# Loading the residual between its first stores, and the values' products four units behind the scores

## The chip, the cores and the metric

The kernel runs on one core of a Trainium2 chip. The metric is the time of one execution in microseconds on the device, here the median of several runs. A second execution under the hardware profiler gives the busy times, waits and clocks that are quoted.

## The reference

A two-layer encoder over 1024 tokens of width 1024, all in float32. The first layer begins with grouped-query attention (16 heads of 64, 4 key/value heads), then come cross-attention into 256 memory tokens and a gated MLP; the second layer has a pooling mixer in place of the attention. Every sub-layer is normed first and added to the residual. The parts that matter here:

```python
def attend_block(q_blk):
    scores = jnp.einsum('bkgqd,bksd->bkgqs', q_blk, kt).astype(jnp.float32)
    p = jax.nn.softmax(scores, axis=-1).astype(vt.dtype)
    return jnp.einsum('bkgqs,bksd->bkgqd', p, vt)
...
x = x + axial_gqa_attention(rmsnorm(x, attn_norm[ia]), attn_w_qkv[ia], ...)
x = x + memory_cross_attention(rmsnorm(x, xattn_norm[i]), rmsnorm(mem, mem_norm[i]), ...)
```

## The kernel before

Matrix products run on TensorE (PE) with every operand split into a high and a low float32r part: ScalarE (ACT) makes the high part by a copy, VectorE (DVE) the low part by a subtraction, and three matmuls (`mm3`, L746 to L748) are added up.

*The attention loop.* There are 128 units, one for each head and each block of 128 queries; two neighbouring units form a pair. Per unit:

- `scores`: four matmuls (L779) into a score buffer `pA` (two of them), the row maximum on DVE (L789), the exponential on ACT (L792), the reciprocal of the sum on DVE (L794) and the scaling of the weights on GpSimd (POOL, L795).
- `turn_p`: eight transposes of the scaled weights on TensorE (L740) into two `pB` buffers (four of them), and the split into `PT` by ACT (L673) and DVE (L674).
- `values`, once a pair: sixteen matmuls (L1192, L1193), a copy on ACT (L1198), a DMA that moves half of it across partitions (`crossed`, L1200), an addition on POOL (L1202) and, for every second pair, two more POOL instructions (L1205, L1206).

`skewed` writes these three stages step by step, each with its lag in units; the tile scheduler then lays out each engine's queue from that program order and from when it holds operands to be ready. In the projection and what follows it the program order is the queue order.

*The loop's end.* The output weight `attn_w_o` is loaded in eight pieces through the `scr` buffers (`load_rows`, `load_w`, L681) that the attention weights also use, and each is split. The residual X (eight row tiles of 128 x 1024) is loaded from the input, 512 KB a tile (L2128). All these DMAs are issued by SP, one after the other; one that has to wait holds up those behind it.

*The projection.* `begin` walks over 16 steps (n, t), n the half of the columns, t the row tile: (0,0), (0,2), (1,0), (1,2), (0,4), (1,4), (0,6), (1,6), (0,1), (1,1), and so on. Each has a product (`gemm`, 24 matmuls), a call of `free(n, t)`, the addition to X on DVE (L1556), and a store of that half tile of X to DRAM (`save`, L314, tensor `Xq`). After the second half of a tile its norm factor is computed on ACT and POOL (L727, L719, L721), and DVE's norm (L318) overwrites X in place, with `gain`, a row broadcast to all partitions (`bcast`, L712). The norm therefore waits for both stores of its tile to land. Between the steps stand the transposes of normed tiles (`turn`, L323): tile 0 behind the product (1,2), tile 2 behind (0,4).

Of the kernel before, what the change touches and what calls it, by code (L numbers as in the profile page):

```python
# [16 lines left out]
P = 128  # L17
# [62 lines left out]
def skewed(n, *stages):  # L80

    for step in range(n + max(lag for lag, _ in stages)):
        for lag, stage in stages:
            if 0 <= step - lag < n:
                stage(step - lag)
# [212 lines left out]
class Seven:  # L298
# [71 lines left out]
    def load(self, f, j):  # L370

        c = self.columns(f)[j]
        src = self.w[:, c:c + P].rearrange("(k p) n -> p k n", p=P)
        self.nc.sync.dma_start(out=self.raws[f][j].rearrange("p (k n) -> p k n", k=NK), in_=src)
# [254 lines left out]
class Kernel:  # L629
# [132 lines left out]
    def attention(self):  # L762
        nc, R, a, tc = self.nc, self.R, self.a, self.tc
# [4 lines left out]
        units = [(j, hh, i) for j in range(NT // 2) for hh in range(NH) for i in range(2)]  # L768
# [401 lines left out]
        with tc.tile_pool(name="at", bufs=1, reuse_waits="tile") as at:  # L1170
            PT = [[at.tile([P, 2048], F32R, name=f"PT{i}{j}") for j in range(2)] for i in range(2)]
            halves = self.scr().rearrange("p (a b c) -> p a b c", a=2, b=2)
            def parts(u):
                return (x.rearrange("p (a b) -> p a b", a=8) for x in PT[u // 2 % 2])

            def turn_p(u):
                ph, pl = parts(u)
                c = slice(u % 2 * P, (u % 2 + 1) * P)
                self.transposed(prs.pop(u), lambda g, p: self.hi_lo(ph[:, 4 * g:4 * g + 4, c], pl[:, 4 * g:4 * g + 4, c], p))

            def values(u):
                j, hh, i = units[u]
                if i == 0:
                    return
                kv = hh // 4
                if hh == 0:
                    OT.append([R.get(), R.get()])
                ph, pl = parts(u)
                o = self.psB()[:, :256]
                for kt in range(NT):  # L1190
                    v = R.tiles[V[kt // 4]].rearrange("p (k h c) -> p k h c", k=4, h=4)[:, kt % 4, kv, :]
                    nc.tensor.matmul(o, v, ph[:, kt], start=kt == 0, stop=False)  # L1192
                    nc.tensor.matmul(o, v, pl[:, kt], start=False, stop=kt == NT - 1)  # L1193
                odd, pair = hh % 2, u // 4 % 2
                if not odd:
                    sums["crossed"] = at.tile([P, 256], F32, name="crossed", bufs=2)
                own, far = halves[:, pair, odd], sums["crossed"]
                nc.scalar.copy(own, o)  # L1198
                mine, other = (slice(HD * odd, HD * odd + HD), slice(HD - HD * odd, P - HD * odd))
                nc.sync.dma_start(out=far[mine], in_=own[other])  # L1200
                total = halves[:, pair, 0]
                nc.gpsimd.tensor_tensor(out=total[mine], in0=own[mine], in1=far[mine], op=OP.add)  # L1202
                if odd:
                    hi, lo = (R.v(x, 8)[:, hh // 2] for x in OT[j])
                    nc.gpsimd.tensor_scalar(hi, total, 1.0, 1.0, op0=OP.mult, op1=OP.mult)  # L1205
                    nc.gpsimd.tensor_tensor(out=lo, in0=total, in1=hi.bitcast(F32), op=OP.subtract)  # L1206
                if hh % 4 == 3:
                    if j % 2:
                        R.put(Q[kv, j // 2])

            skewed(len(units), (0, scores), (2, turn_p), (3, values))
            R.put(*V, *K[0], *K[1])
        return OT

# [5 lines left out]

        return (self.R.hv(h).rearrange("p (k n) -> p k n", k=4)[:, k % 4, cols] for h in hs[k // 4 * 2:k // 4 * 2 + 2])

    def cross(self, i, X, steps=None, mixer=None, over={}):

        nc, R, a = self.nc, self.R, self.a
        Xd = self.tc.dram_tile([S, D], F32, name=f"Xq{i}")
        U = Seven(self, a["xattn_w_q"][i], lambda f: (2 * f * P, (2 * f + 1) * P), X, Xd, self.bcast(a["xattn_norm"][i]))
        plan_sums = self.down_sums(i)  # L1230
        q, nf, mem, kT, v, sm, PT, O, wo = {}, D // (2 * P), {}, [], [], {}, {}, {}, {}
        both = lambda t: [(f"X{t}", j) for j in range(2)]
# [6 lines left out]
        def plan_split(plan, name, f, late):  # L1239
# [3 lines left out]
            def high():  # L1243
                hs = q[c] = R.get_halves(1)
                nc.scalar.activation(R.hv(hs[0]), U.bank[f][name], AF.Copy, scale=XHD ** -0.5)

            def low():
                h, l = (R.hv(x) for x in q[c])
                nc.vector.scalar_tensor_tensor(l, U.bank[f].pop(name), XHD ** -0.5, h.bitcast(F32), op0=OP.mult, op1=OP.subtract)
            ins = [(u, 0), (u, 1)]  # L1250
# [184 lines left out]
        def main():  # L1435
            order = U.order(nf)
            if steps:
                U.begin(*steps, lambda: None)
                U.H["T4"] = [R.get(), R.get()]
                over.update({"DVE": 6.5, "ACT": 4.9})  # L1440
            plan = Plan(R, over, {"scr": 2 if steps else 6, "A": 2, "B": 4, "half": len(R.freed)})
            if mixer:
                mixer(plan, U, X)
                order[:4] = [(2, 0), 3, (1, 0), 5, (2, 1), None]
# [673 lines left out]
    def run(self):  # L2118
        nc, R, a = self.nc, self.R, self.a
        OT = self.attention()  # L2120
        ws = [self.load_rows(a["attn_w_o"][0], 0)]
        xp = self.ctx.enter_context(self.tc.tile_pool(name="xres", bufs=1, reuse_waits="tile"))
        X = [xp.tile([P, D], F32, name=f"X{t}") for t in range(NT)]
        for t in (0, 2, None, 4, 6, 1, 3, 5, 7):
            if t is None:
                ws.append(self.load_rows(a["attn_w_o"][0], 1))
            else:
                nc.sync.dma_start(out=X[t], in_=a["x"][0][t * P:(t + 1) * P, :])  # L2128

        def lhs(t, k):  # L2130
            return (R.v(s, 8)[:, k, t % 4 // 2 * P:(t % 4 // 2 + 1) * P] for s in OT[t // 4 * 2 + t % 2])

        def free(t):
            if t % 4 >= 2:
                R.put(*OT[t // 4 * 2 + t % 2])

        steps = self.rows_by(lhs, X, free, lambda n, k: self.blk(ws[n], k, slice(0, 512)), lambda n: R.put(*ws[n]))
        lhs, *ops = self.cross(0, X, steps)
        ready = []
        gemm, add, over = self.ffn(0, lhs, X, *ops, lambda plan: ready.extend([self.pool_weights(plan)]))  # L2140
        lhs, *ops = self.cross(1, X, None, partial(self.pool_mixer, gemm, add, ready[0]), over)
        self.ffn(1, lhs, X, *ops, out=self.out[0])


# [30 lines left out]
```

## Time and profile before

| | us |
|---|---|
| median of 3 runs | 2509.69 (2505.69 to 2514.07) |
| the profiled execution, its time | 2508.51 |
| its span, first to last instruction | 2506.7 |
| TensorE busy | 2473.4 (99%) |
| VectorE busy | 1958.6 (78%) |
| ScalarE busy | 1348.4 (54%) |
| GpSimd busy | 436.2 (17%) |
| mean granted clock of TensorE | 0.998 |

The times in rows of the profile are microseconds from the first instruction of the span. A row of the timeline has start, duration, engine, line, operation, what is written and read; in brackets stands how long the engine was idle before it and what ended the wait. A row of the waits has who waited for whom, the total, the number of times and the longest. Matmuls overlap in a pipeline, so from one start to the next is the better measure of them than the duration. The attention loop lies between about 175 and 529 us, the projection behind it.

### The profile page before, as it was taken

What the parts mean: (1) busy time and instruction counts of PE and PEld (TensorE: products, weight loads), DVE (VectorE), ACT (ScalarE), POOL (GpSimd) and SP (SyncE); (2) the same over time, 40 slices, a digit from 0 to 9 for tenths busy, and PEclk for the clock granted to TensorE, in tenths of its full rate; (3) what the DMA queues carried; (4) which work ended last, traced back from release to release, by engine and by line L of the source; (5) the groups of instructions that cost most, each with busy time, mean ns of one, the idle gap of its engine ahead of it and who ended that gap; (6) DMA issues with size and microseconds to landing.
All of it is one profiled execution on the core that took longest, in us unless ns stands there. A gap on an engine that the chain in (4) does not pass through costs nothing.

```text
span 2506.7 us, 37225 instructions
## 1 busy us (share of the span) xinstructions
PE 2473.4 (99%) x13435; PEld 2129.7 (85%) x13435; DVE 1958.6 (78%) x2899; ACT 1348.4 (54%) x2307; POOL 436.2 (17%) x594
## 2 busy tenths in 40 slices
PE   9999999999999999999999999999999999999998
PEld 8999999978898888888888888889888888887887
DVE  7779989864986379888889776987559888888875
ACT  6558888852655255555555334655335555554542
POOL 5756666631011000000000003102010000000001
PEclk9999999999999999999999999999999999999999
DMA  7100000042595124243258553388223324337852
GB/s 253 43 2 14 13 14 13 13 171 68 187 317 183 57 79 126 84 122 110 85 170 285 198 182 111 126 283 306 73 72 109 114 84 124 108 93 255 278 189 97
DMA packets 314733, 326.50 MB, mean 130 GB/s; under 512 B 14133, under 2 KB 248861, under 8 KB 314549
## 3 DMA queue, kind: packets, MB, share of 16 engines
q1 hardware_dynamic: 314549, 324.12, 39.9%
q8 instruction: 106, 1.74, 0.3%
q14 instruction: 78, 0.64, 0.1%
HBM read 232.48 MB, written 82.58 MB: 126 GB/s over the span
## 4 chain that ended last, share of the span: by engine, by line
PE 87%; issue 4%; DVE 3%; DMA 2%; ACT 2%; POOL 1%; SPq 0%; POOLq 0%; DVEq 0%; ACTq 0%
PE pB L746 21%; PE pB L748 21%; PE pB L747 21%; PE pA L779 4%; PE pB L740 4%; PE pA L748 3%; PE pA L746 3%; PE pA L747 3%; PE pB L1193 2%; PE pB L1192 2%; DVE R L668 1%; PE pB L323 1%; ACT R L665 1%; DMA scr<-in_ffn_w_down 1%; PE pA L2058 1%
## 5 line engine op out<-in xcount | busy, mean ns | idle before, releaser
L746 PE MATMUL pB<-R,R 128*128 128x512 f32 (+1 forms) x2764 | 1024.3, 371 | 8.4 <-DVE scr L439 3.3
L748 PE MATMUL pB<-R,R 128*128 128x512 f32 (+1 forms) x2760 | 1016.4, 368 | 1.3 <-DVE R L668 1.2
L747 PE MATMUL pB<-R,R 128*128 128x512 f32 (+1 forms) x2764 | 1017.3, 368 | 0.0
L746 PEld LDWEIGHTS pB<-R,R 128*128 128x128 f32 x2764 | 521.1, 189 | 100.7 <-DVE scr L439 4.6
L748 PEld LDWEIGHTS pB<-R,R 128*128 128x128 f32 x2760 | 520.1, 188 | 89.0 <-DVE R L668 2.6
L747 PEld LDWEIGHTS pB<-R,R 128*128 128x128 f32 x2764 | 521.2, 189 | 85.6 <-DVE R L674 0.4
L665 ACT ACTIVATE R<-scr 128x512 fp32r<-128x512 f32 (+2 forms) x340 | 256.9, 781 | 218.3 <-DMA scr<-Gs 60.3
L668 DVE TENSOR_TENSOR R<-scr,R 128x512 fp32r<-128x512 f32 (+2 forms) x340 | 291.6, 887 | 21.5 <-ACT R L665 20.9
L668 DVE TENSOR_TENSOR R<-X,R 128x512 fp32r<-128x512 f32 x374 | 252.5, 686 | 67.5 <-ACT R L665 66.6
L665 ACT ACTIVATE R<-X 128x512 fp32r<-128x512 f32 x374 | 231.7, 630 | 135.8 <-PE pB L747 65.4
L719 POOL TENSOR_SCALAR ms<-ss 128x1 f32<-128x1 f32 (+1 forms) x53 | 14.9, 281 | 1659.0 <-ACT R L727 1280.7
L437 ACT COPY scr<-pB 128x512 f32<-128x512 f32 x156 | 91.3, 585 | 188.3 <-PE pB L748 182.5
L673 ACT ACTIVATE PT<-pB 128x512 fp32r<-128x512 f32 x256 | 140.1, 604 | 56.0 <-PE pB L740 55.7
L789 DVE TENSOR_REDUCE nm<-pA 128x1 f32<-128x1024 f32 x125 | 152.5, 1220 | 20.5 <-PE pA L779 20.5
L674 DVE TENSOR_TENSOR PT<-pB,PT 128x512 fp32r<-128x512 f32 x256 | 163.5, 679 | 5.0 <-ACT PT L673 4.9
L1765 DVE TENSOR_TENSOR X<-pB,X 128x512 f32<-128x512 f32 (+1 forms) x145 | 99.3, 686 | 85.5 <-PE pB L748 84.5
L795 POOL TENSOR_SCALAR scr<-scr,inv 128x1024 f32<-128x1024 f32 x125 | 140.7, 1127 | 70.1 <-DVE inv L794 69.8
L746 PE MATMUL pA<-R,R 128*128 128x512 f32 (+1 forms) x420 | 150.6, 359 | 0.0
L748 PE MATMUL pA<-R,R 128*128 128x512 f32 (+1 forms) x420 | 150.2, 358 | 0.2 <-DVE R L668 0.2
L747 PE MATMUL pA<-R,R 128*128 128x512 f32 (+1 forms) x420 | 150.0, 357 | 0.0
L779 PE MATMUL pA<-R,R 128*128 128x512 f32 x512 | 145.4, 405 | 0.0
L792 ACT ACTIVATE scr<-pA,nm 128x1024 f32<-128x1024 f32 x125 | 139.8, 1118 | 1.5 <-DVE nm L789 0.5
(172 smaller groups left out, 3485.0 us busy)
## 6 DMA issues: line engine op xcount, KB each, us to landing
X<-in_ffn_w_up SPq DMA_DIRECT2D x82, 512.0 KB
Gs<-X SPq DMA_DIRECT2D x105, 256.0 KB
scr<-in_ffn_w_down SPq DMA_DIRECT2D x45, 512.0 KB
scr<-Gs SPq DMA_DIRECT2D x35, 512.0 KB
scr<-in_xattn_w_kv SPq DMA_DIRECT2D x32, 512.0 KB
scr<-Gs SPq DMA_DIRECT2D x42, 384.0 KB
Wt<-scr SPq DMA_DIRECT2D x44, 256.0 KB
Gs<-scr SPq DMA_DIRECT2D x42, 256.0 KB
```

The source lines that it names most:

```text
L665: self.nc.scalar.activation(hi, src, AF.Copy)
L668: self.nc.vector.tensor_tensor(out=lo, in0=src, in1=hi.bitcast(F32), op=OP.subtract)
L673: nc.scalar.activation(hi, src, AF.Copy)
L674: nc.vector.tensor_tensor(out=lo, in0=src, in1=hi.bitcast(F32), op=OP.subtract)
L740: self.nc.tensor.transpose(p[:, k, :], src[:, b * P:(b + 1) * P], self.ident)
L746: mm(out, ah, bh, start=start, stop=False)
L747: mm(out, ah, bl, start=False, stop=False)
L748: mm(out, al, bh, start=False, stop=stop)
L779: nc.tensor.matmul(s[:, kh * 512:(kh + 1) * 512], q, R.v(K[part][kh], 4)[:, kv], start=part == 0, stop=part == 1)
L789: nc.vector.tensor_reduce(nm, s, axis=AX.X, op=OP.max, negate=True)
L792: nc.scalar.activation(pr, s, AF.Exp, bias=nm, accum_out=rs)
L795: nc.gpsimd.tensor_scalar(pr, pr, ri, 1.0, op0=OP.mult, op1=OP.mult)
```

## The change

Two edits. In the loop, `values` stands four units behind the scores instead of three, and within a step it comes before `turn_p`. In the order of the program a pair was scores, transposes, scores, transposes, values; it becomes scores, transposes, scores, values, transposes.

For the residual, tiles 0, 2 and 4 are loaded up front as before (with the gain row now in front of tile 4, where it came behind all loads), and tiles 6, 1, 3, 5 and 7 are loaded one at a time out of `free`, that is between the product of a step and its store: behind the products (1,2), (0,4), (1,4), (1,6) and (0,1). The rest of the diff passes the gain row into `cross`.

```diff
-            skewed(len(units), (0, scores), (2, turn_p), (3, values))
+            skewed(len(units), (0, scores), (4, values), (2, turn_p))
...
-    def cross(self, i, X, steps=None, mixer=None, over={}):
+    def cross(self, i, X, gain, steps=None, mixer=None, over={}):
...
-        U = Seven(self, a["xattn_w_q"][i], lambda f: (2 * f * P, (2 * f + 1) * P), X, Xd, self.bcast(a["xattn_norm"][i]))
+        U = Seven(self, a["xattn_w_q"][i], lambda f: (2 * f * P, (2 * f + 1) * P), X, Xd, gain)
...
-        for t in (0, 2, None, 4, 6, 1, 3, 5, 7):
-            if t is None:
-                ws.append(self.load_rows(a["attn_w_o"][0], 1))
-            else:
-                nc.sync.dma_start(out=X[t], in_=a["x"][0][t * P:(t + 1) * P, :])
+
+        def load(t):
+            nc.sync.dma_start(out=X[t], in_=a["x"][0][t * P:(t + 1) * P, :])
+        load(0)
+        load(2)
+        ws.append(self.load_rows(a["attn_w_o"][0], 1))
+        gain = self.bcast(a["xattn_norm"][0])
+        load(4)
+        later = {(1, 2): 6, (0, 4): 1, (1, 4): 3, (1, 6): 5, (0, 1): 7}
...
-        steps = self.rows_by(lhs, X, free, lambda n, k: self.blk(ws[n], k, slice(0, 512)), lambda n: R.put(*ws[n]))
-        lhs, *ops = self.cross(0, X, steps)
+        gemm, add, freed = self.rows_by(lhs, X, free, lambda n, k: self.blk(ws[n], k, slice(0, 512)), lambda n: R.put(*ws[n]))
+
+        def between(n, t):
+            freed(n, t)
+            if (n, t) in later:
+                load(later[n, t])
+        steps = gemm, add, between
+        lhs, *ops = self.cross(0, X, gain, steps)
...
-        lhs, *ops = self.cross(1, X, None, partial(self.pool_mixer, gemm, add, ready[0]), over)
+        lhs, *ops = self.cross(1, X, self.bcast(a["xattn_norm"][1]), None, partial(self.pool_mixer, gemm, add, ready[0]), over)
```

## The prediction

> **What bounds the kernel now.** I read the page first (busy shares, the chain of waits), then what TensorE waits for over the whole span, then the two places that the change touches, as windows and as instructions in order of time.
>
> ```profile
> span 2506.7 us, 37225 instructions
> PE 2473.4 (99%) x13435; PEld 2129.7 (85%) x13435; DVE 1958.6 (78%) x2899; ACT 1348.4 (54%) x2307; POOL 436.2 (17%) x594
> PE pB L323 <- DVE X L318: 3.9, 2, 3.5
> PE pB L740 <- POOL scr L795: 3.0, 5, 1.0
> ```
>
> TensorE is busy 99% of the span, so an edit without fewer matmuls can win only idle time of TensorE. All its waits are short. The two longest groups that the change can reach are the transposes of the normed residual (L323), which once wait 3.5 us for VectorE's norm, and the transposes of the attention weights (L740), which five times wait for GpSimd's scaling (L795), 3.0 us together. That is the size of the prize: some 7 us, 0.3%, which is also about the least that a measurement of this kernel tells from no change. The half-clock stretch below is the only other loss there.
>
> The windows of the attention loop and of the stretch behind it (columns: stretch, length, then busy time of PE, PEld, DVE, ACT, POOL, then granted clock, DMA share, GB/s) and a list of TensorE's waits from 186 to 516 us:
>
> ```profile
> 281.00:362.00 81.00, 81.00 (x596) 74.44 (x595) 73.41 (x119) 68.65 (x133) 51.72 (x59) 1.00 0.05 13
> 484.00:491.00 7.00, 6.14 (x44) 5.29 (x43) 6.15 (x10) 4.73 (x10) 4.42 (x6) 1.00 0.07 18
> 522.30:525.60 3.30, 1.68 (x11) 1.14 (x10) 1.43 (x3) 1.84 (x4) 1.06 (x2) 1.00 0.41 128
> 525.60:528.80 3.20, 3.20 (x16) 3.20 (x17) 2.81 (x3) 1.51 (x2) 0.69 (x1) 0.50 0.82 305
> 551.00:555.00 4.00, 0.46 (x4) 0.32 (x4) 1.65 (x2) 0.00 (x0) 0.00 (x0) 1.00 0.05 19
> 555.00:640.00 85.00, 85.00 (x408) 70.73 (x405) 45.54 (x63) 33.17 (x62) 7.81 (x16) 1.00 0.20 65
> PE pB L740 <- POOL scr L795: 1.8, 3, 0.9
> ```
>
> In the quiet loop TensorE has no gap and VectorE is busy 91% (73.41 of 81). Three times, as at 484 to 491, TensorE loses up to 0.9 us, 1.8 us in all; then at the loop's end (522.3 to 525.6) it is idle 1.6 of 3.3 us, and the next 3.2 us run at clock 0.50. At 551 to 555 it is idle 3.5 us, in the projection.
>
> One pair of units in order of time (start, duration, engine, line):
>
> ```profile
> 340.05 1.09 PE L779 MATMUL pA<-R,R 128*128 128x512 f32 x4
> 340.99 1.03 PE L740 MATMUL pB<-ident,scr 128*128 128x128 f32 x8
> 341.18 1.23 DVE L789 TENSOR_REDUCE nm<-pA 128x1 f32<-128x1024 f32 x1 [0.35 <-PE pA L779]
> 341.68 1.09 ACT L673 ACTIVATE PT<-pB 128x512 fp32r<-128x512 f32 x2 [0.84 <-PE pB L740]
> 341.77 1.17 PE L779 MATMUL pA<-R,R 128*128 128x512 f32 x4
> 342.32 1.28 DVE L674 TENSOR_TENSOR PT<-pB,PT 128x512 fp32r<-128x512 f32 x2
> 342.79 1.03 PE L740 MATMUL pB<-ident,scr 128*128 128x128 f32 x8
> 342.93 0.73 POOL L1202 TENSOR_TENSOR scr<-scr,crossed 64x256 f32<-64x256 f32 x1 [0.81 <-ACT PT L673]
> 343.52 1.21 DVE L789 TENSOR_REDUCE nm<-pA 128x1 f32<-128x1024 f32 x1
> 343.57 0.36 PE L1192 MATMUL pB<-PT,R 128*128 128x256 f32 x1
> 344.65 0.15 DVE L794 RECIPROCAL inv<-sum 128x1 f32<-128x1 f32 x1
> 344.72 1.27 DVE L674 TENSOR_TENSOR PT<-pB,PT 128x512 fp32r<-128x512 f32 x2
> 344.98 1.12 POOL L795 TENSOR_SCALAR scr<-scr,inv 128x1024 f32<-128x1024 f32 x1
> 345.52 1.10 PE L779 MATMUL pA<-R,R 128*128 128x512 f32 x4
> 346.46 1.03 PE L740 MATMUL pB<-ident,scr 128*128 128x128 f32 x8
> ```
>
> A pair takes 345.52 - 340.05 = 5.47 us: scores (S) 0.94, transposes (T) 0.78, S 1.02, T 0.78, values (V) 1.95. The reader is to see how VectorE follows closely: maximum 341.18, low parts 342.32, maximum 343.52, reciprocal 344.65, low parts 344.72. By these starts its pair of units costs 2 x (1.14 + 1.20 + 0.07) = 4.82 of 5.47 us.
>
> **The change, part by part.** The loop first. It adds no instruction; V moves from behind the second T to in front of it, so TensorE's pair becomes S T S V T.
>
> (1) *The three stalls.* After a V come a copy, a DMA across partitions (L1200) and, every second time, three GpSimd instructions from L1202 on (342.93 to 344.98, 2.05 us); the scaling L795 stands behind them, ends at 346.10, and T needs it at 346.46: slack 0.36. When the DMA is late, the slack is gone:
>
> ```profile
> 487.53 0.73 POOL L1202 TENSOR_TENSOR scr<-scr,crossed 64x256 f32<-64x256 f32 x1 [2.13 <-DMA crossed<-scr]
> 489.57 2.22 POOL L795 TENSOR_SCALAR scr<-scr,inv 128x1024 f32<-128x1024 f32 x2
> ```
>
> After the change, counted from V's end: the three start at 2.88 as now (340.05 to 342.93) and end at 4.93; T and the next first score run until 1.72, and that score's own T stands one pair later, at 1.72 + 5.47 = 7.19, so its scaling (1.12) must start by 6.07. Slack 1.1 instead of 0.36, provided that the second score's scaling is queued ahead of the three. The largest stall, 0.86, then vanishes: -1.8 us (bounds 0 and -1.8).
>
> (2) *The period itself.* With V in front of T, the low parts of that T reach VectorE 1.95 us later against the scores, and VectorE has nothing in the meantime. If the queues hold an order that fits, the period stays 5.47 and this costs 0; if not, see the second rival. No row shows the new order; from both sides: 0 (TensorE has no gap to give) and the chain worked out there, and beyond it one ACT split more. I take 0, because VectorE's total, 4.82, still fits 5.47 and the present order, laid out by readiness, has no wait.
>
> (3) *The loop's start.* The third score of the loop comes 1.95 us earlier, right behind T, and needs the score buffer of unit 3, whose exponential ends at 178.79:
>
> ```profile
> 177.67 1.12 ACT L792 ACTIVATE scr<-pA,nm 128x1024 f32<-128x1024 f32 x1
> 177.72 1.03 PE L740 MATMUL pB<-ident,scr 128*128 128x128 f32 x8
> ```
>
> T ends near 178.6: +0.2 us (0 to 0.4).
>
> (4) *The loop's end.* The last score now runs in front of the V before it, so its scaling is done before its T: the idle 1 us in front of that T goes. What is late next is the output weight, split into high and low parts just as the projection needs it:
>
> ```profile
> 530.77 1.06 ACT L673 ACTIVATE R<-scr 128x1024 fp32r<-128x1024 f32 x1 [0.41 <-DMA scr<-in_attn_w_o]
> 531.87 1.47 DVE L674 TENSOR_TENSOR R<-scr,R 128x1024 fp32r<-128x1024 f32 x1 [0.25 <-ACT R L673]
> 533.39 0.50 PE L747 MATMUL pB<-R,R 128*128 128x512 f32 x1
> ```
>
> The matmul at 533.39 starts when the low part (531.87 + 1.47 = 533.34) is there, and that waited for its DMA, which is issued when the last T frees its buffer. So of 1.6 us idle and 1.6 us lost to the clock (half of 3.2), about what that T moves forward is won: -1.0 (bounds 0 and -3.2).
> [...]
>
> Now the loads. Five of eight loads of X leave the head of SP's queue; each now stands behind a store that waits for VectorE's addition.
>
> ```profile
> X<-in_x SPq DMA_DIRECT2D x8, 512.0 KB
> 530.00:551.00 21.00, 21.00 (x93) 16.85 (x91) 9.58 (x9) 6.82 (x8) 3.49 (x5) 1.00 0.95 363
> 545.75 0.69 DVE L1556 TENSOR_TENSOR X<-pB,X 128x512 f32<-128x512 f32 x1 [2.01 <-PE pB L748]
> 553.35 1.28 DVE L318 SCALAR_TENSOR_TENSOR X<-X,rs,scr 128x1024 f32<-128x1024 f32 x1 [6.91 <-DMA Xq<-X]
> 554.69 1.09 PE L323 MATMUL pB<-ident,X 128*128 128x128 f32 x8 [3.54 <-DVE X L318]
> 557.43 1.28 DVE L318 SCALAR_TENSOR_TENSOR X<-X,rs,scr 128x1024 f32<-128x1024 f32 x1 [2.19 <-POOL rs L721]
> ```
>
> (5) *The stall.* The addition ends at 546.4, its store lands only at 553.3 because the DMA engines are full (share 0.95) with X; the norm, which overwrites X in place, waits 6.9 us, TensorE 3.54. Five loads are 2.6 MB, at 363 GB/s 7 us: without them the engines are empty by 544, before the store is issued. An undisturbed store lands within the 2.2 us that the norm at 557.43 waits for its scale anyway. So the norm runs 548.7 to 550.0, and TensorE wants it at 551.15: -3.5 us (bounds -3.5 and -2).
>
> (6) *The moved loads.* X6 is issued at about 547, three products and two transposes before the addition that uses it; the other four have four products or more. Each load adds 1.4 us (512 KB at 363 GB/s) in front of the next store. DMA share from 555 to 640 is 0.20, which hides them: 0; without that cover a norm would come 1.4 us later, five times, against 2 us that TensorE leaves it (bounds 0 and +1). The gain row's load, now ahead of X4, and X4 itself are needed after 548: 0. In the second layer the same load is only written elsewhere: 0.
>
> Sum: -1.8 + 0 + 0.2 - 1.0 - 3.5 + 0 = -6.1 us. The profiled execution took 2508.5 us (span 2506.7), so 2502.4; the median of the runs shown is 1.2 higher, and I put the forecast between: 2503.
>
> **The rivals.** *More at the loop's end.* If the weight's loads move up with the transposes, term (4) is worth 3.2 rather than 1.0: 2500.5. For it: the half clock has no other visible cause than the gap in front of it. Against it: the low part at 531.87 waits for a DMA.
>
> *The loop gets longer* (the other side). If VectorE keeps its order (maximum, low parts, maximum, reciprocal), a chain closes over two pairs: maximum 1.14, low parts 1.20, maximum 1.13, to the scaling 0.33, scaling 1.12, T 0.78, S 0.98 (the mean of 0.94 and 1.02), V 1.95, to the high parts 0.69 (340.99 to 341.68), to the low parts 0.64, low parts 1.20 = 11.16 us against 2 x 5.47 = 10.94. That is 0.11 a pair; with some 63 pairs +7 us, and the net is +1: 2510. If an exponential (1.1 us) also lands ahead of the high parts in ACT's queue, the chain has 12.3, 0.66 a pair at worst; an engine that slips only partly gives 0.2 to 0.3, +13 to +19, net +7 to +13: 2516 to 2522. Break-even is 6.1 / 63 = 0.10 a pair, and 0.22 makes it slower by 0.3%. For it: VectorE is busy 91% and the pair now leaves it without work during V. Against it: a reciprocal queued ahead of the second maximum, or high parts ahead of the exponential, breaks the chain.
>
> *The stores still wait.* If a store and its load behind it share the engines instead of following each other, term (5) shrinks to -2 and (6) costs 1: 2505.5. Against it: the store at 546.4 was late by what stood in front of it.
>
> **How the numbers follow.** Forecast 0.45 (2499 to 2506); more at the end 0.10; stores still wait 0.07; loop longer by about 0.1 a pair 0.15; by 0.2 or more 0.23. Faster by over 0.3% (under about 2502): all of the second and four in ten of the first, 0.28. Slower by over 0.3% (over 2517): most of the last, and no other, 0.22, and 0.02 for what I do not see. Within: 0.48. The range 2498 to 2519 leaves out half of the last case and the lower edge of the second.
>
> **What would show it.** TensorE's wait at L323 for L318 gone (5), and X6 landed long before its addition (6). In the loop, pairs of 5.47 us with no wait of L740 for L795 (1, 2); a low clock missing near 526 (4); the projection's first matmul at about 526 and a wait for the weight's low part behind it. I am wrong if pairs take 5.6 us or more and TensorE's waits for VectorE or ACT appear in every pair.

## The result, and the profile after

| | median, us | range | ratio to before, 95% interval |
|---|---|---|---|
| before | 2511.08 | 2505.69 to 2514.21 | 1 |
| after | 2516.63 | 2513.91 to 2518.41 | 1.0024 [1.0016, 1.0031] |

Forecast 2503: the change was to win 6.1 us, and it loses 5.5. The time lies within the range given, on the side of the rival "the loop gets longer". The profiled execution of after took 2517.59 us, 1.0 above its median; that of before took 2508.51, 2.6 below its own. So the traces show 9.1 us between the two, and the medians 5.5.

From the page of after:

```profile
span 2515.8 us, 37288 instructions
PE 2480.7 (99%) x13435; PEld 2134.8 (85%) x13435; DVE 1963.1 (78%) x2899; ACT 1346.1 (54%) x2307; POOL 434.1 (17%) x594
...
PE 83%; DVE 4%; POOL 4%; DMA 3%; issue 3%; ACT 2%; SPq 0%; POOLq 0%; DVEq 0%; ACTq 0%
```

TensorE's waits over the whole span (what waited, for what, us in total, times, longest):

```profile
PE pB L740 <- POOL scr L795: 8.0, 30, 0.5
```

The window of the quiet loop (columns as in the prediction's windows), in before and in after:

```profile
285.00:480.00 195.00, 194.44 (x1418) 178.02 (x1417) 176.18 (x284) 163.50 (x320) 126.79 (x143) 1.00 0.05 13
285.00:480.00 195.00, 190.28 (x1365) 173.22 (x1364) 171.44 (x272) 157.31 (x307) 120.07 (x137) 1.00 0.05 13
```

The five waits of the transposes (L740) for GpSimd's scaling (L795) have become thirty, one in every second pair, and on the page 4% of the chain that ended last now lies on GpSimd and 3% on DMA (1% and 2% in before). GpSimd is busy 17% of the span. In the window from 285 to 480 us TensorE is idle 4.7 of 195, in before 0.6.

Where the time went, by setting the matmuls of the two traces side by side one for one (after minus before, us; in the loop, where the orders differ, V stands against the same V, and the one score, 0.98, that after has done more by then is taken off):

| place (time in before) | change |
|---|---|
| up to the loop, and its first turn (to 191) | 0.0 (-0.5 ahead of the loop, +0.5 at its start) |
| attention loop (191 to 506) | +11.6 |
| loop's end, projection's start (506 to 540) | -1.4 |
| projection with the first stores (540 to 556) | -3.8 |
| everything behind (556 to the end) | +2.5 |

In the loop the time between two values (V) was 5.47 us in before; in after it alternates between 5.5 and 5.9, two pairs in 11.42 us instead of 10.94. Here is one such round of two pairs in the chain of waits of after (start, duration, what; left out are V's matmuls from 345.46 to 347.35 and the pieces of 0.1 us and less between the steps):

```profile
338.43 0.75 POOL scr L1202
...
339.26 0.40 POOL R L1205
...
339.74 0.74 POOL R L1206
340.49 1.12 POOL scr L795
...
341.65 1.09 PE pB L740 x8
342.74 0.93 PE pA L779 x4
343.67 0.87 PE pB L740 x8
344.54 0.92 PE pA L779 x4
...
347.37 0.38 ACT scr L1198
...
347.77 1.92 DMA crossed<-scr
...
349.85 0.74 POOL scr L1202
```

The chain starts and ends at the same instruction, 11.42 us apart (349.85 - 338.43): it is closed. GpSimd joins the crossed halves (three operations), scales, TensorE then runs T S T S V, ScalarE copies, the DMA crosses, and GpSimd joins again. Nothing in it is long; it is only that every step waits for the one before. GpSimd's instructions in order of time show where the scaling stands:

```profile
338.43 0.74 POOL L1202 TENSOR_TENSOR scr<-scr,crossed 64x256 f32<-64x256 f32 x1 [1.67 <-DMA crossed<-scr]
339.26 0.40 POOL L1205 TENSOR_SCALAR R<-scr 128x256 fp32r<-128x256 f32 x1
339.74 0.74 POOL L1206 TENSOR_TENSOR R<-scr,R 128x256 fp32r<-128x256 f32 x1
340.46 2.23 POOL L795 TENSOR_SCALAR scr<-scr,inv 128x1024 f32<-128x1024 f32 x2
```

And from the list of all engines, the reciprocal that the scaling needs and the transposes that need the scaling:

```profile
338.89 0.15 DVE L794 RECIPROCAL inv<-sum 128x1 f32<-128x1 f32 x1
...
341.65 0.33 PE L740 MATMUL pB<-ident,scr 128*128 128x128 f32 x1 [0.27 <-POOL scr L795]
```

The reciprocal is done at 339.04. The scaling starts at 340.46, behind the three, and a second one behind it (x2). GpSimd had sat idle 1.67 us for the crossing transfer just before. TensorE waits 0.27 us by the bracket. By the starts it is more: these transposes start 0.55 behind V's last matmul, where 0.12 is usual, and the next score starts 0.85 behind them, where 0.79 is usual (the rows are in the last section). Together that is the 0.48 that a round is longer, give or take 0.01.

### The profile page after: what moved, and what is told of

Read it like the earlier page. It is cut to its first block, busy times and chain, and to the rows that moved or that the text cites. A ratio compares the mean times of both kernels' runs of the same rounds, so it can differ in the third digit from the quotient of the medians.

```text
span 2515.8 us, 37288 instructions
## 1 busy us (share of the span) xinstructions
PE 2480.7 (99%) x13435; PEld 2134.8 (85%) x13435; DVE 1963.1 (78%) x2899; ACT 1346.1 (54%) x2307; POOL 434.1 (17%) x594
## 4 chain that ended last, share of the span: by engine, by line
PE 83%; DVE 4%; POOL 4%; DMA 3%; issue 3%; ACT 2%; SPq 0%; POOLq 0%; DVEq 0%; ACTq 0%
PE pB L746 21%; PE pB L748 21%; PE pB L747 21%; PE pA L748 3%; PE pA L746 3%; PE pA L747 3%; PE pB L740 3%; PE pA L779 3%; DMA crossed<-scr 2%; POOL scr L795 1%; DVE R L668 1%; PE pB L1193 1%; PE pB L1192 1%; PE pB L323 1%; POOL R L1206 1%
## 5 line engine op out<-in xcount | busy, mean ns | idle before, releaser
L795 POOL TENSOR_SCALAR scr<-scr,inv 128x1024 f32<-128x1024 f32 x125 | 139.6, 1124 | 51.3 <-DVE inv L794 51.3
L740 PE MATMUL pB<-ident,scr 128*128 128x128 f32 x1024 | 134.5, 274 | 9.3 <-POOL scr L795 8.0
```

Of the source, the lines that this page charges most:

```text
L740: self.nc.tensor.transpose(p[:, k, :], src[:, b * P:(b + 1) * P], self.ident)
L795: nc.gpsimd.tensor_scalar(pr, pr, ri, 1.0, op0=OP.mult, op1=OP.mult)
```

## The experiments

Theory A: this closed chain, through GpSimd's queue, sets the loop's time. The rivals: VectorE and ScalarE close a chain of their own (D, the mechanism that the prediction gave for a longer loop), a lag of four units is too long in itself (C), the moved loads cost something (B).

All ratios are against before; the last column is the median distance from one V to the second next, in one profiled execution. Before was run again beside the experiments and had medians of 2510.1 to 2511.0 there, so a difference of 1 us between two rows is not read.

| run | us | ratio, 95% interval | two pairs, us |
|---|---|---|---|
| loads only | 2504.14 | 0.9979 [0.9970, 0.9987] | 10.96 |
| loop only | 2520.72 | 1.0047 [1.0034, 1.0059] | 11.42 |
| values behind the transposes | 2508.47 | 0.9997 [0.9988, 1.0006] | 10.96 |
| after, join behind | 2501.30 | 0.9966 [0.9955, 0.9978] | 10.95 |
| before's loop, loads, join behind | 2501.04 | 0.9962 [0.9949, 0.9974] | 10.96 |
| after without the crossing | 2500.21 | 0.9957 [0.9943, 0.9971] | 10.95 |
| after, L1205 twice | 2507.44 | 0.9988 [0.9978, 0.9997] | 11.12 |
| the same, order held | 2532.70 | 1.0091 [1.0074, 1.0107] | 11.91 |

**The two parts of the change, each alone.** After with the loop's order of before:

```diff
-            skewed(len(units), (0, scores), (4, values), (2, turn_p))
+            skewed(len(units), (0, scores), (2, turn_p), (3, values))
```

> The five moved loads and the earlier gain, with the attention loop in the order of before (values three units behind). Theory A (the time is lost in the attention loop, by its order alone; the store stall behind the loop is saved as predicted): pairs of 5.47 us, the stall of 3.5 to 3.8 us gone, so 3 to 4 us under before, ratio about 0.9986. Rival B (the moved loads cost something in the loop or later, by the queues they share with the crossing transfers): pairs longer than 5.5 us, and no less than before in the sum, ratio 1.000 or more.

And the loop's new order with the loads and `cross` as in before:

```diff
-            skewed(len(units), (0, scores), (2, turn_p), (3, values))
+            skewed(len(units), (0, scores), (4, values), (2, turn_p))
```

> Only the loop's new order (values four units behind, queued ahead of the transposes of two units behind); the loads stand where they stood in before. Theory A: the whole loss is here, pairs of 5.70 us instead of 5.47 from the first to the last, some 11 to 12 us in the loop, 1.6 us of it back at the loop's end, the store stall of 3.5 us still there: about 10 us over before, ratio 1.004. Rival B: pairs of at most 5.55 us, within 4 us of before.

The loads alone win 6.0 us by the medians (the traces: 3.7; 3.8 at the store, 1.2 at the loop's end, less 1.3 elsewhere), the loop alone loses 10.6. Rival B is out: with the loads alone pairs keep 5.47 us. The instructions around before's wait for the store, in order of time, tell which half wins there. With the loads only (norm, transposes):

```profile
548.84 1.29 DVE L318 SCALAR_TENSOR_TENSOR X<-X,rs,scr 128x1024 f32<-128x1024 f32 x1 [2.71 <-DMA Xq<-X]
...
550.68 1.03 PE L323 MATMUL pB<-ident,X 128*128 128x128 f32 x8
```

With the loop only:

```profile
564.31 1.97 PE L323 MATMUL pB<-ident,X 128*128 128x128 f32 x8 [3.35 <-DVE X L318]
```

With the loads moved the transposes wait for nothing; with only the loop changed they still wait 3.35 us (they then take 1.97 us, where with the loads moved they take 1.03). The loop's loss is the loop's alone.

**Is it the lag or the place?** After with V four units behind, but queued after the transposes of its step, so that TensorE's round is S T V S T:

```diff
-            skewed(len(units), (0, scores), (4, values), (2, turn_p))
+            skewed(len(units), (0, scores), (2, turn_p), (4, values))
```

> After, with the products with the values still four units behind the scores but queued behind the transposes of their step instead of ahead of them, so TensorE runs T of a unit, then V, then S and T of the next. Theory A (a closed chain V, copy L1198, crossing transfer, three GpSimd operations L1202 L1205 L1206, scaling L795, transposes, which V has to wait out because it stands ahead of two transposes): V then stands where it stood in before against the scalings, the chain opens, pairs of 5.47 to 5.50 us; with the store stall gone 3 to 5 us under before, ratio about 0.9985. Rival C (a lag of four is itself too long, whatever the place, since probabilities and their halves are held for one unit more): pairs stay at 5.65 to 5.70, 5 us over before, ratio 1.002.

Pairs are 5.47 again by the median, so the lag of four isn't what lengthens every pair, and C falls as it was put. The time, 2508.5, is some 2 us over what A gave. (One of the eleven executions took 5037.9 us; the ratio leaves it out, and no trace shows what happened in it.) Six scattered waits are left, larger than the three of before:

```profile
PE pB L740 <- POOL scr L795: 3.9, 6, 1.2
```

With them the mean pair between 186 and 516 us is 5.59 us, against 5.52 in before and 5.72 in after. Why they are larger than in before isn't settled. In this profile another 2.9 us against before were lost ahead of the loop, where the granted clock of the first 100 us was 0.98 rather than 1.00; the edit changes nothing in that stretch.

**Take the join out of the scaling's way.** The three operations of GpSimd are moved to a step of their own, queued behind the scaling of the unit five behind; V, loads and the number of instructions stay as in after:

```diff
+            def join(u):
+                ...
+                behind = scaled.get(u + 5)
+                with tc.issue_after(behind) if behind is not None else nullcontext():
+                    nc.gpsimd.tensor_tensor(out=total[mine], in0=own[mine], in1=far[mine], op=OP.add)
+                    ...
-            skewed(len(units), (0, scores), (4, values), (2, turn_p))
+            skewed(len(units), (0, scores), (5, join), (4, values), (2, turn_p))
```

> After, with one edit: the three GpSimd operations that join the crossed halves (L1202 L1205 L1206 of after, here L1214 L1216 L1217) are queued behind the scaling of the unit five behind, so a scaling no longer stands behind them in GpSimd's queue while they wait for the crossing transfer. Theory A (the queue of GpSimd closes the chain): no wait of L740 for L795 of more than 0.2 us, pairs of 5.47 to 5.50, so the 12 us of the loop come back: some 5 us under before, ratio 0.998. Rival D (VectorE and ScalarE close the chain: they stand still while V runs, and then maximum, reciprocal, scaling and transposes follow one another): pairs stay at 5.6 to 5.7, about 5 us over before, ratio 1.002.

2501.3 us, 15.3 less than after by the medians, and more than the 12 us of the loop; the next experiment tells why. The window of the loop:

```profile
285.00:480.00 195.00, 195.00 (x1427) 181.10 (x1427) 179.81 (x285) 164.69 (x322) 126.34 (x143) 1.00 0.05 14
```

And GpSimd in order of time:

```profile
338.27 1.13 POOL L795 TENSOR_SCALAR scr<-scr,inv 128x1024 f32<-128x1024 f32 x1 [0.26 <-DVE inv L794]
340.18 1.12 POOL L795 TENSOR_SCALAR scr<-scr,inv 128x1024 f32<-128x1024 f32 x1 [0.78 <-DVE inv L794]
341.26 0.73 POOL L1214 TENSOR_TENSOR scr<-scr,crossed 64x256 f32<-64x256 f32 x1
343.74 1.14 POOL L795 TENSOR_SCALAR scr<-scr,inv 128x1024 f32<-128x1024 f32 x1 [1.74 <-DVE inv L794]
```

TensorE has no gap in 195 us, and every scaling now waits for its reciprocal only; no join waits for its transfer. VectorE is busy 179.81 of 195, 92%, with V standing where after has it. VectorE's instructions stand in the order of after (maximum, reciprocal, three low parts, reciprocal, maximum, low part), and so do ScalarE's. So D is out: the order S T S V T closes no chain through these two that is longer than TensorE's own work.

**The same edit in before's loop.** The loads as in after, the loop's order of before, the join behind as above:

```diff
-            skewed(len(units), (0, scores), (2, turn_p), (3, values))
+            skewed(len(units), (0, scores), (5, join), (2, turn_p), (3, values))
```

> The loads as in after, the loop's order of before (values three units behind, queued behind the transposes), and the three GpSimd operations that join the crossed halves queued behind the scaling of the unit five behind. Theory A (the three stalls of before, 1.0 us each, came from the same thing as the long pairs of after, a scaling behind a join that waits for a late crossing transfer): the stalls go here too, pairs 5.47, 2.5 to 3 us less than with the loads alone, so 8 to 9 us under before, ratio 0.9966, as with values four behind and the same edit; the lag of the values then makes no difference. Rival E (it was the lag of four that took the three stalls away): as with the loads alone, 6 us under before, ratio 0.998.

2501.0 us, 3.1 less than the loads alone, and in this trace the transposes wait for the scaling nowhere between 186 and 516 us. The three stalls of before had the same cause as the long pairs of after, and with the join out of the way the two orders of V can't be told apart (0.9962 and 0.9966). These two are the fastest versions that compute everything.

**Break the chain somewhere else.** After without the crossing transfer; the queue of GpSimd keeps its length:

```diff
-                nc.sync.dma_start(out=far[mine], in_=own[other])
-                nc.gpsimd.tensor_tensor(out=total[mine], in0=own[mine], in1=far[mine], op=OP.add)
+                nc.gpsimd.tensor_tensor(out=total[mine], in0=own[mine], in1=own[mine], op=OP.add)
```

> After without the crossing transfer: L1202 adds an own half to itself instead of the half that crossed, so the halves of the heads are not joined (that part of the output is left out); the number and the order of all other operations is that of after. Theory A (closed chain of 11.42 us over two pairs, 1.92 + 0.16 us of it the transfer and the wait for it): the chain drops to about 9.3 us, under the 10.94 that TensorE needs for two pairs, so pairs of 5.47, 12 to 14 us less than after, 2503, ratio to before 0.997. Rival D (VectorE and ScalarE close the chain): the transfer is not on it, pairs stay at 5.6 to 5.7, 2514 or more, ratio 1.001 to 1.002.

2500.2 us, 16.4 less than after, where A gave 12 to 14; the three stalls of before are gone here too:

```profile
285.00:480.00 195.00, 195.00 (x1429) 181.12 (x1428) 179.81 (x285) 164.64 (x320) 122.66 (x144) 1.00 0.01 1
```

Without those 64 KB transfers, whose engines are 5% busy in the loop, TensorE again has no gap. It is their latency in the chain (1.92 us in the round above) that costs, not their bytes.

**Lengthen the chain by a known amount.** First L1205 was simply issued twice in after:

```diff
                     nc.gpsimd.tensor_scalar(hi, total, 1.0, 1.0, op0=OP.mult, op1=OP.mult)
+                    nc.gpsimd.tensor_scalar(hi, total, 1.0, 1.0, op0=OP.mult, op1=OP.mult)
```

> After with L1205 (0.40 us of GpSimd, once per two pairs) issued twice in a row with the same result: a known amount more on the suspected chain, while GpSimd is idle most of the time. Theory A: the chain over two pairs grows from 11.42 to 11.82 us, pairs from 5.71 to 5.91 us, 0.20 us more for each of some 57 pairs, so 11 us over after: 2528, ratio to before 1.0067. Rival D (VectorE and ScalarE close the chain; GpSimd's queue has slack): pairs stay at 5.70, 2517, ratio 1.0024.

Neither came: with an instruction more, the kernel became 9 us faster than after. GpSimd in order of time shows why:

```profile
335.16 0.74 POOL L1202 TENSOR_TENSOR scr<-scr,crossed 64x256 f32<-64x256 f32 x1 [1.67 <-DMA crossed<-scr]
335.99 0.41 POOL L1205 TENSOR_SCALAR R<-scr 128x256 fp32r<-128x256 f32 x1
336.48 0.41 POOL L1206 TENSOR_SCALAR R<-scr 128x256 fp32r<-128x256 f32 x1
336.87 1.13 POOL L795 TENSOR_SCALAR scr<-scr,inv 128x1024 f32<-128x1024 f32 x1
337.96 0.73 POOL L1207 TENSOR_TENSOR R<-scr,R 128x256 fp32r<-128x256 f32 x1
...
346.27 0.74 POOL L1202 TENSOR_TENSOR scr<-scr,crossed 64x256 f32<-64x256 f32 x1 [1.66 <-DMA crossed<-scr]
```

The order in this queue isn't written out in the loop, and with one operation more it came out otherwise: the scaling stands ahead of the last of the join's operations (L1207). From the join's start to the scaling's start it is 1.71 us instead of 2.03, so the chain is 0.32 shorter, 11.10; the row of the next round is at 346.27, 11.11 later. The edit tested something else than it was made for; worked out afterwards for the order that came, A gives the period that was measured.

So the edit was made again with each scaling held behind the join that it stood behind in after:

```diff
+        def scale(u):
+            ...
+            behind = joined.get(u - 4)
+            with tc.issue_after(behind) if behind is not None else nullcontext():
+                nc.gpsimd.tensor_scalar(pr, pr, ri, 1.0, op0=OP.mult, op1=OP.mult)
-            skewed(len(units), (0, scores), (4, values), (2, turn_p))
+            skewed(len(units), (0, scores), (4, values), (0, scale), (2, turn_p))
```

> The run before this one issued L1205 twice, but GpSimd's queue came out in another order (one scaling stands ahead of the last of the join's operations instead of behind it), so it didn't test the longer chain. Here L1205 is issued twice and each scaling is held behind the join that it stood behind in after, so GpSimd's queue is that of after with one operation more per two pairs, 0.49 us from its start to the start of the next. Theory A (closed chain of 11.42 us over two pairs): 11.91 us over two pairs, 5.95 a pair, 0.24 us more for each of some 57 pairs, 14 us over after: 2530, ratio to before 1.0076. Rival D (VectorE and ScalarE close the chain): pairs of 5.70 as in after, 2517, ratio 1.0024. Rival F (the chain of GpSimd has slack that the shorter order merely happened to enlarge): pairs between 5.70 and 5.80.

2532.7 us against the 2530 that A gave, 16 over after. TensorE's waiting transposes in two rounds, one behind the other (the lines of the scaling have moved to L803):

```profile
336.89 1.09 PE L740 MATMUL pB<-ident,scr 128*128 128x128 f32 x8 [0.75 <-POOL scr L803]
...
348.80 1.09 PE L740 MATMUL pB<-ident,scr 128*128 128x128 f32 x8 [0.74 <-POOL scr L803]
```

348.80 - 336.89 = 11.91 us, as worked out; the wait of 0.27 in after has become 0.75, by the 0.49 that the operation adds. Rival F, a queue with slack in it, is out too.

Wherever the chain was worked out (after 11.42, without the crossing 9.3, L1205 twice 11.10, order held 11.91), the time of two pairs, scattered waits aside, is the larger of 10.95 us, TensorE's own work, and the length of the closed chain. The loop-only run, which has after's loop, has after's 11.42; the others stand at 10.95 or 10.96. That is shown, and with it the loss of after.

## Why the prediction was wrong

**(1), the failed step.** It counted 1.1 us of slack "provided that the second score's scaling is queued ahead of the three". It isn't: the row at 340.46 shows both scalings behind them. The scaling that comes first behind the three isn't the one whose transposes are due at 7.19 us after V's end but the one before it, due at 7.19 - 1.72 = 5.47. The prediction's own numbers then give: the three end at 4.93, the scaling at 6.05, 0.58 us late. Moving V in front of the transposes takes one score (S, 0.94) from between V and those transposes, so the slack of 0.36 becomes -0.58, not +1.1. Measured were 0.48 us for two pairs, over the whole loop +11.6 instead of -1.8. The proviso was named, but it was left out of the rivals; the order of GpSimd's queue in before (the rows at 342.93 and 344.98 stood in the prediction) already showed a scaling behind the join. The sign that it gave for being wrong came by half: pairs of 5.7 us, but with a wait for GpSimd in every second one and not for VectorE or ACT in each. And its bound of 1.8 us for the three stalls, read from the idle times, was too small: before's mean pair of 5.52 instead of 5.47 makes 3 us over 60 pairs, and 3.1 came back with the join behind.

**(2), the period.** The wait of VectorE and ScalarE behind V was priced as the danger. The runs with the join behind and without the crossing show that V's new place costs them nothing: 195 us without a gap. So the 0 was right for what (2) spoke of. The rival that took it up, "the loop gets longer", named a time of 2516 to 2522 and pairs 0.2 to 0.3 longer, which is what came (2516.6; 0.24 a pair), but by the wrong chain: the 11.16 us through the low parts do not close, the 11.42 through GpSimd's join do. In the order that came, a reciprocal (340.79) stands ahead of the maximum (340.89), which the prediction had named as what breaks its chain.

**(3), the loop's start:** +0.2 expected with a bound of 0.4, some 0.45 seen: ahead of the loop after lies 0.47 us in front of before, and by 190 us no longer. More than half is one wait for a score buffer, as (3) had it, but a pair later than it said. The weights of the score at 183.88 wait for the exponential:

```profile
183.87 0.77 PEld L779 LDWEIGHTS pA<-R,R 128*128 128x128 f32 x4 [0.26 <-ACT scr L792]
```

**(4), the loop's end:** -1.0 expected, -1.4 in the trace, within its bounds, but by luck. Some 1.2 us of before's loss there was a half clock (0.50 from 525.60 to 528.80 us) that is gone in the loads-only run too (1.00 from 526.50 to 529.70), where the loop's order is that of before. So most of what (4) shows as won can't be credited to the order (more below). The idle 1 us in front of the last T did go; in its place the last V waits 1.33 us for ScalarE's split of that T, which stands in the queue behind the split of a piece of the output weight that waits for its load:

```profile
535.30 1.06 ACT L673 ACTIVATE R<-scr 128x1024 fp32r<-128x1024 f32 x1 [1.23 <-DMA scr<-in_attn_w_o]
537.17 0.38 PE L1192 MATMUL pB<-PT,R 128*128 128x256 f32 x1 [1.33 <-ACT PT L673]
```

**(5), the store:** -3.5 expected; -3.8 in after and with the loads alone. The rows of after answer to those of before at 545.75, 553.35 and 554.69:

```profile
555.92 0.69 DVE L1556 TENSOR_TENSOR X<-pB,X 128x512 f32<-128x512 f32 x1 [3.87 <-PE pB L748]
...
559.17 1.29 DVE L318 SCALAR_TENSOR_TENSOR X<-X,rs,scr 128x1024 f32<-128x1024 f32 x1 [2.55 <-DMA Xq<-X]
...
561.17 1.03 PE L323 MATMUL pB<-ident,X 128*128 128x128 f32 x8
```

The norm starts 2.6 us after the addition's end (2.3 was worked out), and the transposes no longer wait. The norm's wait for its store, 2.55 us, is 0.4 over the neighbouring norm's 2.2 from which it was estimated.

**(6), the moved loads:** 0, as expected. From 540 to 680 us VectorE's longest waits are these, and none of its waits is for a load of X from the input:

```profile
DVE X L1556 <- PE pB L748: 22.5, 13, 3.9
DVE X L318 <- POOL rs L721: 9.0, 4, 2.3
```

Behind 556 the traces drift apart by 2.5 us, most of it between 1320 and 1582 us. The change edits nothing in that stretch, the loads alone show none of it, the join-behind run 1.5. In after 1.35 us of it come at one place, around 1585 us, where the clock is 0.50 and before's is 1.00 (the rows are in the last section); in the join-behind run 1.3 of the 1.5 come at the same place. Why the clock falls there, and where the rest comes from, was not tried.

## What to carry to other kernels

When an instruction is moved on one engine, look at the queues that its result ends in, and ask what stands behind it there and when that is due (here a scaling whose reciprocal was done at 339.04 us started at 340.46, behind the join); an engine that is busy 17% can still set the time by its order. Close the chain over one whole round and compare it with the busiest engine's work: here the round took the longer of the two, 11.42 us against 10.95, and a chain that is 0.5 us over costs that in every round. And an order that is put out by a planner is not held by leaving it alone: one operation more changed it here and won 9 us, so an experiment on a queue has to fix the order that it wants to test.

## What the runs showed of the hardware

*The half clock* does not follow from the idleness in front of it alone in these traces. At the loop's end of before TensorE is idle 1.6 of 3.3 us, and then the clock is 0.50 for 3.2 us; the prediction saw no other cause for that than this gap. The loads-only run has the same stretch 0.9 us later, with the same busy time (1.68 of 3.30 us), and keeps its full clock:

```profile
523.20:526.50 3.30, 1.68 (x12) 1.09 (x10) 1.42 (x4) 1.79 (x4) 1.07 (x1) 1.00 0.42 140
526.50:529.70 3.20, 3.20 (x21) 2.92 (x22) 2.94 (x3) 2.60 (x4) 0.73 (x1) 1.00 0.88 323
```

In front of the transposes of the normed residual the loop-only run waits 3.35 us, and from their start to that of the next matmul it is then 1.62 us (564.31 to 565.93). Before waits 3.54 us at the same place, and there it is 0.85 (554.69 to 555.54), at a clock of 1.00. So the loop-only run went at about half speed there, an estimate from these starts. And in after the clock falls once behind a stretch in which TensorE was not idle at all:

```profile
1579.50:1583.40 3.90, 3.90 (x35) 3.77 (x33) 2.62 (x4) 3.43 (x7) 0.74 (x2) 1.00 0.30 127
1583.45:1586.85 3.40, 3.40 (x18) 3.40 (x18) 0.74 (x2) 0.00 (x0) 0.00 (x0) 0.50 0.00 0
```

At the same place of the program (1576.00 to 1579.40 us) before keeps 1.00.

What sets the low clock no run here shows; the one behind the busy stretch of after stays open. A gain of 1.2 us that hangs on it belongs in a range, not in a sum.

*The idle time in brackets was less than the wait cost.* It is counted from the end of the matmul before, but matmuls overlap, so an undisturbed one starts before that end (347.17 against 347.05 + 0.28 below). In after, first the transposes that wait for the scaling (with the last matmul of V in front of them and the score behind), then the next ones behind a V, which don't:

```profile
341.10 0.27 PE L1193 MATMUL pB<-PT,R 128*128 128x256 f32 x1
341.65 1.09 PE L740 MATMUL pB<-ident,scr 128*128 128x128 f32 x8 [0.27 <-POOL scr L795]
342.50 1.17 PE L779 MATMUL pA<-R,R 128*128 128x512 f32 x4
...
347.05 0.28 PE L1193 MATMUL pB<-PT,R 128*128 128x256 f32 x1
347.17 1.04 PE L740 MATMUL pB<-ident,scr 128*128 128x128 f32 x8
347.96 1.18 PE L779 MATMUL pA<-R,R 128*128 128x512 f32 x4
```

From V's last start to the score's it is 1.40 us with the wait and 0.91 without: the wait of 0.27 us in brackets cost 0.49.
